# A two-layer hybrid trunk on one core: values and next scores of the samples in one stretch, spatial weights turned by VectorE, probabilities scaled by ScalarE

## The chip, the cores and the metric

The kernel runs as one program on one core of a Trainium2 chip. The metric is the device time of one execution in microseconds (us). The engines are named as in the profile: PE is TensorE (PEld its weight loads), DVE is VectorE, ACT is ScalarE, POOL is GpSimd, SP is SyncE, which issues most DMA transfers. Each engine works through its own list of instructions in order.

## What is computed

One inference step of a trunk with two layers, for a prompt (512 rows of 1024) and eight samples (16 rows each), all fp32. Layer 0 is a gated MLP whose mixing over positions works in blocks of 128 for the prompt and, for a sample, with the top left 16 x 16 of the same weights:

```
uv = gelu(h @ w_in[:, :2E]);  z = h @ w_in[:, 2E:]           # E = 2048
v  = layer_norm(uv[:, E:])
wm = where(chunk_causal, w_s[:, :n, :n], 0)                   # 16 groups, n = 128 or 16
s  = einsum('gij,bnjgc->bnigc', wm, v) + b_s
y  = (u * s * silu(z)) @ w_out
```

Layer 1 is attention with 16 heads of 128 and a cumulative forget bias. The prompt attends to itself; a sample attends to 256 cached rows and its own 16 rows:

```
s = q @ k.T * scale + c_q - c_k          # c = cumsum of log forget values
p = softmax(mask(s));  o = p @ v;  y = (o * silu(z)) @ w_out
```

Each layer ends with a norm, the residual, and a gated input embedding. Keys, values and log forget values of the new rows are outputs too.

## The kernel before

The 640 rows (512 of the prompt, 128 of the samples) are kept channel-major as two fp32r parts, high and low, and each large product is three fp32r products (lines 272 to 274): high by high, high by low, low by high. Weights are fetched into RAW tiles, and ACT writes the high part (line 289), DVE the low part (line 290, by subtraction). Many large products are done by a seven-product scheme (`seven_products`) whose sums of weights POOL makes (line 211).

Layer 0: panels of v (to about 120 us of the span), then eight pairs of channel groups (about 120 to 350 us). A pair g, g+1 runs the seven products for u, then `spatial_weights(g)` and `spatial_weights(g + 1)`, then the seven products for z, then `gate_spatial`, which multiplies v by the turned spatial weights. In `spatial_weights` the 128 x 128 weights of a group (`raw`) are turned by PE and copied by ACT into `wm` (lines 688, 690, 691). For the samples, DVE builds a matrix `ax` with the group's 16 x 16 weights (`w16`) eight times along the diagonal, PE turns it (line 689), and ACT copies it into `ws` (line 692). Behind every second of the first three pairs' ends, and before the first, a panel of v is normalised by ACT and DVE (`layer_norm_panel`).

Layer 1: eight rounds, one per pair of heads p. `interleave` walks through the seven-product steps of the next projections (z of p; v, k, q of p+1); a step adds 0.441 to a clock, and a piece of the attention of pair p is written into the program when the clock passes the number beside it. `sample_times`, `prompt_times` and `attention_pieces` are those tables. Behind them a scheduler of the compiler moves instructions within each engine's list by its own estimates; `tc.issue_after(x)` ties what is issued inside it behind x.

The samples' attention of a round goes in two groups `bg` of four samples. The pieces of a group: `scores` (eight products of 128 rows x 32 columns, four samples side by side on the four quarters of PE's columns, then the weighing: DVE adds the bias and takes the minimum, ACT the exponential, DVE the reciprocal and the masked copy of the new rows), `turn` (PE turns the probabilities), `values` (twelve such products, in the order of three key blocks t and four samples), `gate` (PE turns the output, DVE multiplies by z). The two groups use the same buffers: `pr` for probabilities and, over it, `os_` for the output; `kt` for keys and `vv` for values. `load_v(p, 1)` loads the values of the second group (512 KB twice) over those of the first. `bank(ATT)` hands out three PSUM banks in turn (4, 5, 6) to all attention pieces. `turn_v` turns the new values of the next pair (line 1071) into such banks.

The prompt's attention of a head has four query blocks, each with `scores`, `turn` (7.5 later), `values` (12.5 later). In `scores`, ACT takes the exponential (line 1175), DVE the reciprocal (line 1179), and DVE scales the probabilities (line 1180); `turn` has PE turn them (line 1186). `SML` holds one-column values; most are given out from a ring of 20, in layer 1 from a larger one.

## Time and profile before

| | |
|---|---|
| median of three runs | 1273.82 us (1273.16 to 1274.09) |
| profiled execution: its time | 1273.51 us |
| profiled execution: its span | 1271.6 us |
| PE busy | 1264.2 us (99%) |
| DVE busy | 957.1 us (75%) |
| ACT busy | 594.6 us (47%) |
| POOL busy | 356.2 us (28%) |
| granted TensorE clock | 1.000 |

The span runs from the first to the last instruction; what the time has beyond it (1.9 us) lies around it. The page lists groups of instructions by line of the kernel, engine, operation and tile, with the busy time, the mean of one in ns, and what ended the engine's idle time before them. A matmul's duration there reaches beyond the start of the next one, since matmuls are pipelined. In an order of time, a row has the start, the length from the first start to the last end of the merged rows, the engine, and how many records were merged. An fp32 product shows as two records, an fp32r product and a transpose as one.

### The profile page before, as it was taken

The numbers are of one execution on the slowest core, as the hardware profiler recorded it, in microseconds if no ns is written. First come the engines' busy times: TensorE is split into PE (matmuls) and PEld (weight loads), VectorE is DVE, ScalarE is ACT, GpSimd is POOL, SyncE is SP. The second block draws the span as 40 slices with busy tenths as digits, with TensorE's granted clock in tenths as the row PEclk, the third lists the DMA queues.
The fourth block names the chain that finished last, engine by engine and source line by source line (L and its number), as shares of the span: only waits on it lengthen the run. The fifth ranks groups of instructions, "written<-read, shape, count | busy, mean of one in ns | idle before, by whom it ended". The sixth has DMA issues, their size and how long they took to land.

```text
span 1271.6 us, 21433 instructions
## 1 busy us (share of the span) xinstructions
PE 1264.2 (99%) x8038; PEld 1136.5 (89%) x8038; DVE 957.1 (75%) x1795; ACT 594.6 (47%) x1076; POOL 356.2 (28%) x323
## 2 busy tenths in 40 slices
PE   9999999999999999999999999999999999999998
PEld 7888999999988888889999999999999998788887
DVE  6844999999953364789988998989898988545643
ACT  4433555544545343665445454545454445454331
POOL 1012445454000010145434535454435430000100
PEclk9999999999999999999999999999999999999999
DMA  5532343323324212657798858677888659632211
GB/s 201 174 98 78 108 127 112 103 80 104 114 94 144 94 44 84 150 127 157 173 167 168 195 150 186 157 172 142 151 168 179 177 110 283 230 129 84 67 66 50
DMA packets 275545, 171.54 MB, mean 135 GB/s; under 512 B 188721, under 2 KB 238689, under 8 KB 275442
## 3 DMA queue, kind: packets, MB, share of 16 engines
q1 hardware_dynamic: 261170, 127.80, 36.9%
q0 software_dynamic: 9760, 36.05, 13.7%
q10 hardware_dynamic: 4512, 6.33, 1.7%
q8 instruction: 63, 1.03, 0.3%
q14 instruction: 40, 0.33, 0.1%
HBM read 148.55 MB, written 21.59 MB: 134 GB/s over the span
## 4 chain that ended last, share of the span: by engine, by line
PE 97%; DVE 2%; issue 0%; ACT 0%; ACTq 0%; DVEq 0%
PE pb L272 27%; PE pb L274 27%; PE pb L273 27%; PE pb L1193 3%; PE pb L1270 2%; PE pb L419 2%; PE pb L1186 1%; PE pb L1243 1%; PE pb L317 1%; PE pb L745 1%; PE pb L1058 1%; DVE W L290 1%; PE pb L1071 1%; PE pb L1262 0%; PE pb L1059 0%
## 5 line engine op out<-in xcount | busy, mean ns | idle before, releaser
L272 PE MATMUL pb<-A,W 128*128 128x320 f32 (+1 forms) x752 | 240.7, 320 | 0.0
L273 PE MATMUL pb<-A,W 128*128 128x320 f32 (+1 forms) x752 | 233.7, 311 | 0.0
L274 PE MATMUL pb<-A,W 128*128 128x320 f32 (+1 forms) x752 | 233.2, 310 | 0.0
L290 DVE TENSOR_TENSOR W<-RAW,W 128x1024 fp32r<-128x1024 f32 (+1 forms) x122 | 149.6, 1227 | 71.9 <-ACT W L289 69.7
L273 PE MATMUL pb<-W,A 128*128 128x512 f32 x498 | 194.5, 391 | 0.0
L272 PE MATMUL pb<-W,A 128*128 128x512 f32 x498 | 194.5, 393 | 0.0
L274 PE MATMUL pb<-W,A 128*128 128x512 f32 x498 | 194.3, 391 | 0.0
L289 ACT ACTIVATE W<-RAW 128x1024 fp32r<-128x1024 f32 (+1 forms) x122 | 115.8, 949 | 90.0 <-PE pb L274 43.9
L272 PEld LDWEIGHTS pb<-A,W 128*128 128x128 f32 x752 | 141.6, 188 | 1.0 <-issue 0.2
L273 PEld LDWEIGHTS pb<-A,W 128*128 128x128 f32 x752 | 141.6, 188 | 0.5
L274 PEld LDWEIGHTS pb<-A,W 128*128 128x128 f32 x752 | 141.2, 188 | 0.0
L272 PE MATMUL pb<-tbf,W 128*128 128x320 f32 x360 | 118.9, 330 | 0.4 <-DVE R L1099 0.4
L303 POOL TENSOR_TENSOR SML<-SML 128x1 f32<-128x1 f32 x20 | 14.9, 749 | 350.9 <-DVE SML L301 346.2
L274 PE MATMUL pb<-tbf,W 128*128 128x320 f32 x360 | 111.3, 309 | 0.0
L273 PE MATMUL pb<-tbf,W 128*128 128x320 f32 x360 | 111.2, 309 | 0.0
L274 PEld LDWEIGHTS pb<-W,A 128*128 128x128 f32 x498 | 93.4, 188 | 19.6 <-issue 0.4
L273 PEld LDWEIGHTS pb<-W,A 128*128 128x128 f32 x498 | 93.6, 188 | 18.7
L272 PEld LDWEIGHTS pb<-W,A 128*128 128x128 f32 x498 | 93.5, 188 | 18.5
L211 POOL TENSOR_TENSOR sff<-RAW 128x512 f32<-128x512 f32 x46 | 61.2, 1330 | 169.3 <-DVE W L290 90.7
L713 DVE TENSOR_TENSOR R<-R,pb 128x320 f32<-128x320 f32 x184 | 86.3, 477 | 12.8 <-PE pb L274 11.7
L290 DVE TENSOR_TENSOR A<-R,A 128x640 fp32r<-128x640 f32 (+1 forms) x42 | 35.5, 880 | 57.8 <-ACT A L289 57.8
L272 PEld LDWEIGHTS pb<-tbf,W 128*128 128x128 f32 x360 | 67.7, 188 | 10.3 <-issue 5.8
(270 smaller groups left out, 2842.2 us busy)
## 6 DMA issues: line engine op xcount, KB each, us to landing
RAW<-in_fox_w_in POOLq DMA_DIRECT2D x46, 512.0 KB, 7.5
RAW<-in_gmlp_w_in SPq DMA_DIRECT2D x40, 512.0 KB
R<-in_cache_fox_k SPq DMA_DIRECT2D x128, 128.0 KB
R<-in_cache_fox_v SPq DMA_DIRECT2D x32, 512.0 KB
RAW<-in_gmlp_w_out SPq DMA_DIRECT2D x16, 512.0 KB
RAW<-in_ple_w_gate SPq DMA_DIRECT2D x16, 512.0 KB
RAW<-in_fox_w_out SPq DMA_DIRECT2D x16, 512.0 KB
R<-in_fox_w_in POOLq DMA_DIRECT2D x14, 512.0 KB, 8.5
```

The lines of the kernel that those rows point to most:

```text
L211: nc.gpsimd.tensor_tensor(out=o, in0=a, in1=b, op=op)
L272: nc.tensor.matmul(out, lh, rh, start=start, stop=False)
L273: nc.tensor.matmul(out, lh, rl, start=False, stop=False)
L274: nc.tensor.matmul(out, ll, rh, start=False, stop=stop)
L289: first = nc.scalar.activation(out=hi, in_=src, func=AF.Copy)
L290: nc.vector.tensor_tensor(out=lo, in0=src, in1=f(hi), op=ALU.subtract)
L303: behind["pool"] = nc.gpsimd.tensor_tensor(out=q, in0=t, in1=mhalf, op=ALU.pow)
L317: behind["pe"] = nc.tensor.transpose(out=b[:, j * P:(j + 1) * P], in_=src[:, (4 * c + j) * P:(4 * c + j + 1) * P], identity=ident)
L419: line[e] = make(*args, **kw)
L713: behind["dve"] = nc.vector.tensor_tensor(out=into(i, j), in0=a, in1=b, op=ALU.add)
L1193: nc.tensor.matmul(O[:, d], v[:, j, hh * P:(hh + 1) * P], pt[:, j * P:(j + 1) * P], start=(j == 0), stop=(j == i))
L1270: last = nc.tensor.matmul(O[32 * bl:32 * bl + 32, :256], pt[:, t * P + 32 * bl:t * P + 32 * bl + 32], v_of(p)[:, 4] if t == 2 else vv[:, b ...
```

## The change

Three edits.

1. Spatial weights of the samples: the 16 x 16 weights of all groups are loaded twice side by side (16 loads instead of 8), turned once for all groups by DVE, which turns blocks of 32 x 32, and the upper left of each block is copied by ACT into `w16`. `spatial_weights` then multiplies the turned weights by the block mask straight into `ws`; the transpose of `ax` and the copy behind it are gone.
2. Samples: `scores` is split into `products` (PE) and `weigh` (the rest). In rounds 0 to 6, `values` of group 0 moves to the time of the second group's scores and issues the second group's `products` in the same tied sequence; gate, `weigh` and `turn` of the second group follow. `load_v(p, 1)` moves from 18.5 to 26.1, `turn_v` from 26.0 and 27.0 to 28.7 and 29.7. The reciprocal gets a column of its own in `SML`. Round 7 keeps its order.
3. Prompt: the probabilities are scaled by ACT instead of DVE.

```diff
@@ spatial weights
+    twice, turned_twice = r1(o_u, 512), r1(o_u + 512, 512)
     for b in range(NB):
-        dma(w16[b * TS:(b + 1) * TS], w_s[0, :, :TS, :TS].rearrange("g i j -> i g j"))
+        for z in range(2):
+            dma(twice.rearrange("p (g z j) -> z p g j", g=16, z=2)[z, b * TS:(b + 1) * TS], w_s[0, :, :TS, :TS].rearrange("g i j -> i g j"))
+    with queued("dve"):
+        nc.vector.transpose(out=turned_twice, in_=twice)
+    nc.scalar.activation(out=w16, in_=turned_twice.rearrange("p (g z i) -> p g z i", g=16, z=2)[:, :, 0], func=AF.Copy)
...
-            out=ax.rearrange("p (b j) -> p b j", b=NB), in0=blk.rearrange("p (b j) -> p b j", b=NB),
+            out=ws.rearrange("p (b j) -> p b j", b=NB), in0=blk.rearrange("p (b j) -> p b j", b=NB),
...
-        nc.tensor.transpose(out=b[:, P:2 * P], in_=ax, identity=ident)
...
-        nc.scalar.activation(out=ws, in_=b[:, P:2 * P], func=AF.Copy)
@@ prompt scores
-            nc.vector.tensor_scalar(out=pr[:, :n], in0=pr[:, :n], scalar1=ri, scalar2=None, op0=ALU.mult)
+            nc.scalar.activation(out=pr[:, :n], in_=pr[:, :n], func=AF.Copy, scale=ri)
@@ samples
-        def scores():
-            S = bank(ATT)
+        def products(stack):
+            S = kept["S"] = bank(ATT)
+            for hh in range(2):
+                for bl in range(4):
+                    last = nc.tensor.matmul(S[32 * bl:32 * bl + 32, :272], qpads[:, hh, 4 * bg + bl].rearrange("p h q -> p (h q)"),
+                                            kt[:, hh, bl], start=(hh == 0), stop=(hh == 1))
+                    stack.enter_context(tc.issue_after(last.ins))
+
+        def weigh():
+            S = kept["S"]
...
-        def values():
+        def values(follow=None):
             O = bank(ATT)
             with ExitStack() as stack:
...
+                if follow is not None:
+                    follow(stack)
...
+        if p == 7:
+            return [(s0, scores), (s0 + 7.5, turn), (s0 + 12.5, values), (s0 + 17.5, gate),
+                    (s1, scores1), (s1 + 7.5, turn1), (s1 + 12.5, values1), (s1 + 17.5, gate1)]
+        return [(s0, scores), (s0 + 7.5, turn), (s1, lambda: values(products)), (s1 + 2.5, gate), (s1 + 2.6, weigh),
+                (s1 + 7.5, turn1), (s1 + 12.5, values1), (s1 + 17.5, gate1)]
...
-                   (s0 + kb + 0.1, lambda: new_k(p, 1)), (s0 + 13.5, lambda: load_v(p, 1))]
+                   (s0 + kb + 0.1, lambda: new_k(p, 1)), ((s0 + 13.5 if p == 7 else s1 + 0.1), lambda: load_v(p, 1))]
...
-        pieces += [(26.0, lambda p=p: turn_v(p + 1, 0)), (27.0, lambda p=p: turn_v(p + 1, 1))]
+        pieces += [(28.7, lambda p=p: turn_v(p + 1, 0)), (29.7, lambda p=p: turn_v(p + 1, 1))]
```

How the built programs stand on PE is shown at three places. First, a round of layer 1 (the second one) before, where the first group's values stand: line 1270 is the values, line 1186 the turning of a prompt block's probabilities, lines 272 to 274 the large products, `pb_N` a PSUM bank.

```order
L274 MATMUL pb_71<-A,W 128x320
L1270 MATMUL pb_74<-R_69 32x256 x4
L1186 MATMUL pb_76<-CST,R_69 128x128 x2
L1270 MATMUL pb_74<-R_69 32x256 x8
L272 MATMUL pb_72<-tbf,W 128x320
```

The same round before, some 70 rows later, where the second group's scores stand (line 1243; line 1193 is the prompt's values, line 1071 `turn_v`):

```order
L274 MATMUL pb_72<-A,W 128x320
L1193 MATMUL pb_77<-R_69 128x128 x3
L1243 MATMUL pb_74<-R_69 32x272 x8
L1071 MATMUL pb_75<-CST,R_69 128x128 x4
L272 MATMUL pb_73<-tbf,W 128x320
```

And that round now, where both stand together (line 1282 is the values, 1244 the scores, 1189 the turning, 1196 the prompt's values):

```order
L274 MATMUL pb_72<-A,W 128x320
L1282 MATMUL pb_75<-R_69 32x256 x10
L1189 MATMUL pb_74<-CST,R_69 128x128 x4
L1282 MATMUL pb_75<-R_69 32x256 x2
L1244 MATMUL pb_76<-R_69 32x272 x8
L272 MATMUL pb_72<-A,W 128x320
L273 MATMUL pb_72<-A,W 128x320
L274 MATMUL pb_72<-A,W 128x320
L1196 MATMUL pb_77<-R_69 128x128 x3
```

The values moved to the scores' place. They were cut after four by two transposes and are cut after ten by four now; the eight scores follow the last two values with nothing between, in all of rounds 0 to 6. `turn_v` (line 1074 now) stands later, twice four transposes into banks 74 and 76, the second of which is the scores' bank.

In layer 0, one of sixteen places where the transpose of the samples' weights stood, as a difference:

```order
 L273 MATMUL pb_71<-A,W 128x320
 L274 MATMUL pb_71<-A,W 128x320
-L689 MATMUL pb_74<-CST,R_69 128x128
 L272 MATMUL pb_71<-A,W 128x320
 L273 MATMUL pb_71<-A,W 128x320
```

The row is gone, and nothing takes its place on PE.

More of the change, by code (lines that the diff above doesn't have):

```diff
@@ L74, in hybrid_trunk @@
     CST = sbuf.tile([P, C_N], F32, name="CST")
-    SML = sbuf.tile([P, N_SMALL], F32, name="SML")
+    SML = sbuf.tile([P, N_SMALL + 2], F32, name="SML")
     R1 = sbuf.tile([P, N_R1], F32, name="R1")
@@ L681, in spatial_weights @@
         z = g % 2
-        raw, wm, ws, ax = r1(o_wsr + z * P, P), r1(o_wm + z * P, P), r1(o_ws + z * P, P), r1(o_ax, P)
+        raw, wm, ws = r1(o_wsr + z * P, P), r1(o_wm + z * P, P), r1(o_ws + z * P, P)
         nc.vector.scalar_tensor_tensor(out=spb[z], in0=spb[z], scalar=lnb[:, g:g + 1], in1=r1(o_bs + z * P, P), op0=ALU.mult, op1=ALU.add)
         nc.vector.tensor_tensor(
-            out=ax.rearrange("p (b j) -> p b j", b=NB), in0=blk.rearrange("p (b j) -> p b j", b=NB),
+            out=ws.rearrange("p (b j) -> p b j", b=NB), in0=blk.rearrange("p (b j) -> p b j", b=NB),
             in1=w16[:, g:g + 1, :].broadcast_to([P, NB, TS]), op=ALU.mult)
@@ L1235, in sample_pieces @@
         kept = {}
-        def scores():
-            S = bank(ATT)
+        def products(stack):
[7 more added lines that the diff above has]
+            S = kept["S"]
             with queued("dve"):
                 nc.vector.tensor_tensor(out=Wc[:, PAST:], in0=Wc[:, PAST:], in1=CST[:, C_M16:C_M16 + TS], op=ALU.add)
-            for hh in range(2):
-                for bl in range(4):
-                    nc.tensor.matmul(S[32 * bl:32 * bl + 32, :272], qpads[:, hh, 4 * bg + bl].rearrange("p h q -> p (h q)"),
-                                     kt[:, hh, bl], start=(hh == 0), stop=(hh == 1))
-            m, sm, ri = small(), small(), small()
+            m, sm, ri = small(), small(), SML[:, N_SMALL + bg:N_SMALL + bg + 1]
             nc.vector.tensor_tensor_reduce(out=pr[:, :272], in0=S[:, :272], in1=Wc, scale=1.0, scalar=3e38, op0=ALU.add,
@@ L1263, in turn, with scores @@
             nc.scalar.activation(out=pt, in_=tb[:, :384], func=AF.Copy)
-        def values():
+        def scores():
+            with ExitStack() as stack:
+                products(stack)
+            weigh()
+        def values(follow=None):
             O = bank(ATT)
@@ L1285, in gate @@
                                                op0=ALU.mult, op1=ALU.mult)
-        return scores, turn, values, gate
+        return scores, turn, values, gate, products, weigh
     def prompt_times(h, t0, step):
@@ L1296, in prompt_times, with sample_times @@
         return res
-    def sample_times(p, bg, t0):
-        scores, turn, values, gate = sample_pieces(p, bg)
-        return [(t0, scores), (t0 + 7.5, turn), (t0 + 12.5, values), (t0 + 17.5, gate)]
+    def sample_times(p, s0, s1):
+        scores, turn, values, gate, _, _ = sample_pieces(p, 0)
+        scores1, turn1, values1, gate1, products, weigh = sample_pieces(p, 1)
+        if p == 7:
[3 more added lines that the diff above has]
+                (s1 + 7.5, turn1), (s1 + 12.5, values1), (s1 + 17.5, gate1)]
     def store_y(h):
@@ L1319, in attention_pieces @@
         s0, t0 = 5, 4
-        pieces = sample_times(p, 0, s0) + sample_times(p, 1, s1)
+        pieces = sample_times(p, s0, s1)
         ka, kb = 5, 17.6
         pieces += [(s0 + ka, lambda: turn_k(p, 1, 0)), (s0 + ka + 0.1, lambda: load_k(p, 1, 1)), (s0 + kb, lambda: turn_k(p, 1, 1)),
-                   (s0 + kb + 0.1, lambda: new_k(p, 1)), (s0 + 13.5, lambda: load_v(p, 1))]
+                   (s0 + kb + 0.1, lambda: new_k(p, 1)), ((s0 + 13.5 if p == 7 else s1 + 0.1), lambda: load_v(p, 1))]
         for hh in range(2):
```

## The prediction

> **What bounds the kernel now.** I read the page's busy times first, then a table by stage, then what TensorE waits for, and last the order of time around the places that the change touches.
>
> ```profile
> PE 1264.2 (99%) x8038; PEld 1136.5 (89%) x8038; DVE 957.1 (75%) x1795; ACT 594.6 (47%) x1076; POOL 356.2 (28%) x323
> 120.00:350.00 230.00, 229.53 (x1583) 226.78 (x1582) 215.44 (x337) 119.41 (x218) 93.52 (x61) 1.00 0.35 109
> 575.00:1052.00 477.00, 477.00 (x3645) 447.18 (x3644) 421.94 (x974) 229.70 (x456) 214.13 (x207) 1.00 0.77 164
> PEld pb L272 <- DVE R L726: 1.3, 3, 0.4
> ```
>
> The two window rows are the gMLP products (120 to 350 us) and the seven attention rounds (575 to 1052 us); after the length stand the busy times of PE, PEld, DVE, ACT and POOL, then the clock, the DMA share and GB/s. PE is busy for 229.53 of 230 and for 477.00 of 477 us at full clock. So the path is TensorE's own list of instructions: an instruction taken off it shortens the kernel, one put on it lengthens it, and a lighter VectorE by itself gives nothing. VectorE is the next one (215.44 of 230, 421.94 of 477), so a late VectorE is the way to lose. A busy PE can hide an array that is slowly fed; therefore I price everything from the distance between starts, not from durations.
>
> **Edit 1: spatial weights turned by VectorE.** It takes 16 transposes off TensorE (line 689) and 16 copies off ScalarE (line 692).
>
> ```profile
> 143.54 0.31 PE L272 MATMUL pb<-tb,W 128*128 128x320 f32 x1
> 143.98 0.31 PE L272 MATMUL pb<-A,W 128*128 128x320 f32 x1
> 144.13 0.27 PE L689 MATMUL pb<-CST,R 128*128 128x128 f32 x1
> 144.53 0.31 PE L272 MATMUL pb<-A,W 128*128 128x320 f32 x1
> L689 PE MATMUL pb<-CST,R x16: 270/270/272, 140.8 to 336.4; 128*128 128x128 f32 x16
> L692 ACT ACTIVATE R<-pb x16: 277/278/280, 141.6 to 338.0; 128x128 f32<-128x128 f32 x16
> ```
>
> From 143.54 to 143.98 three products take 0.44 us (0.147 each); from 143.98 to 144.53 three products and one transpose take 0.55. A transpose thus costs 0.11 us, not its 0.27 of duration, and 16 of them 1.8 us. The copies (16 x 0.278 = 4.4 us) come off a ScalarE that is busy 119 of 230 us and give nothing by themselves.
>
> What it adds:
>
> ```profile
> 62.80 1.82 SPq L124 DMA_DIRECT2D R<-in_gmlp_w_s  x4
> 69.45 0.33 SPq L124 DMA_DIRECT2D R<-in_gmlp_b_s  x1
> 75.53 0.38 SPq L124 DMA_DIRECT2D RAW<-in_gmlp_w_in  x1
> 125.61 0.16 DVE L649 SCALAR_TENSOR_TENSOR SML<-SML 128x1 f32<-128x1 f32 x1 [0.66 <-POOL SML L303]
> L1219 DVE STREAM_TRANSPOSE R<-R x128: 395/403/444, 559.7 to 1074.9; 128x256 f32<-128x256 f32 x128
> L1085 DVE STREAM_TRANSPOSE R<-R 128x640 f32<-128x640 f32 x16 | 13.3, 831 | 0.0
> ```
>
> Eight more loads on SP's queue at 1.82/4 = 0.46 us are 3.6 us; that queue is free from 69.8 to 75.53, so the weight load behind them stays on time, and the data are there some 50 us before VectorE wants them near 125 us. One VectorE transpose of 128x512 lies between the 128x256 row (0.40) and the 128x640 row (0.83): about 0.7 us, once, standing before the last statistics, where VectorE had 0.66 us idle. If that cover is gone it is 0.7 us in all. The ScalarE copy of 128x256 is less than half a microsecond beside PE's products. Taken: 0, with 0 to 0.7 for the range.
>
> The weight loads of PE wait in this stage three times for VectorE behind the normalisation panels, 1.3 us in all (the wait quoted first). The VectorE work there is the same and starts from PE, so it moves along with PE. At worst each of the three swallows the 0.2 us that its pair of transposes gave (0.7 us in all). Taken: 0.
>
> **Edit 2: values and next scores in one stretch.** Both are products on a quarter of the array (128*32), four side by side.
>
> ```profile
> 667.70 0.31 PE L274 MATMUL pb<-A,W 128*128 128x320 f32 x1
> 667.94 0.64 PE L1270 MATMUL pb<-R 128*32 128x256 f32 x8
> 668.51 0.44 PE L1186 MATMUL pb<-CST,R 128*128 128x128 f32 x2
> 668.88 1.07 PE L1270 MATMUL pb<-R 128*32 128x256 f32 x16
> 669.88 0.41 PE L272 MATMUL pb<-tbf,W 128*128 128x320 f32 x1
> 670.13 0.31 PE L273 MATMUL pb<-tbf,W 128*128 128x320 f32 x1
> ...
> 681.88 1.12 PE L1243 MATMUL pb<-R 128*32 128x272 f32 x16
> 682.94 0.66 PE L1071 MATMUL pb<-CST,R 128*128 128x128 f32 x4
> 699.85 1.50 PE L1270 MATMUL pb<-R 128*32 128x256 f32 x24
> 701.28 0.41 PE L272 MATMUL pb<-tbf,W 128*128 128x320 f32 x1
> ```
>
> A product here is two records, so x24 is twelve products, six passes deep on each of the four column groups. By starts, x8 lasts 0.57, x16 1.00 and x24 1.43 us: 0.215 a pass and 0.14 once per stretch. Going in costs 0.24 - 0.15 = 0.09. Coming out, the first big product is 0.25 - 0.15 = 0.10 longer. Between two stretches stand two transposes of 0.11 in 0.37 us, 0.15 too many, of which 0.09 is the way in again, so coming out into a transpose costs 0.06. A stretch that ends in transposes is therefore 0.09 + 0.14 + 0.06 = 0.29 us beside its passes. The scores at 681.88 are such a stretch (1.06 us, four passes of 0.23).
>
> Before, a round has five stretches: scores, four values, eight values, scores, values. The new order has four, as the scores of the second group stand right behind the values: 0.29 us saved in each of seven rounds. But the tie does not keep other work out: the values are cut after ten, four transposes come in, and two values follow. Before, the cut lay after four, one value per column group. After ten, groups 0 and 1 have three values (six passes), groups 2 and 3 two; the transposes need the whole array, so they wait for six passes. Behind them groups 2 and 3 still owe two passes each, and their scores stand behind these, while groups 0 and 1 have scores alone: six passes instead of four. Is it the longest group that counts? The forget logits show it:
>
> ```profile
> 540.85 0.84 PE L968 MATMUL pb<-R,WF 128*32 128x128 f32 x24
> 541.63 1.09 PE L317 MATMUL pb<-CST,R 128*128 128x128 f32 x8
> ```
>
> By line 968's loop these twelve products are three of 128 columns in group 3, two each in groups 0 and 1, five of 64 in group 2. With a pass of 128 columns at half of 0.215, group 3 takes 6 x 0.108 = 0.65, plus 0.14 = 0.79 us; the rows show 0.78. The even share would be 0.63. So the longest group sets the end, and the cut costs 2 x 0.215 = 0.43 us a round. Net 0.43 - 0.29 = 0.14 longer, seven times 1.0 us. The eighth round is not tied.
>
> The Trainium skill, "TensorEngine Tiling (Array Packing)", section "Key Properties", says that a change of tiling mode drains the engine; the rows agree with the price just read. Counting changes alone by that rule, the edit would be worth -7 x 0.29 = -2.0 us instead of +1.0; that is the second rival below.
>
> Moved with it: the values' load of the second group (1 MB) is now issued behind the next pair's keys.
>
> ```profile
> R<-in_cache_fox_v SPq DMA_DIRECT2D x32, 512.0 KB
> 669.98 0.94 SPq L124 DMA_DIRECT2D R<-in_cache_fox_v  x2
> 677.99 9.01 SPq L124 DMA_DIRECT2D R<-in_cache_fox_k  x4
> 687.10 3.20 SPq L124 DMA_DIRECT2D out<-R  x5
> ```
>
> On this clock it leaves near 687.1 rather than 669.98, and is read at 699.85: 12.7 us. At the stage's 164 GB/s 1 MB takes 6.4 us, so 6 us are left; sharing the engines with another 1 MB of weights it would take all of them. Taken: 0; late by at most 1 us a round. Behind it on SP stand the stores of values and the next keys, which move back by about 1 us of issue; these keys are turned 12 of the planner's units after their load.
>
> **Edit 3: probabilities scaled by ScalarE.**
>
> ```profile
> L1180 DVE TENSOR_SCALAR R<-R,SML 128x128 f32<-128x128 f32 (+1 forms) x64 | 36.4, 568 | 0.8
> L1175 ACT ACTIVATE R<-R,SML 128x128 f32<-128x128 f32 (+1 forms) x64 | 35.7, 558 | 73.8 <-DVE SML L1172 73.8
> L1188 ACT ACTIVATE R<-pb 128x128 f32<-128x128 f32 (+1 forms) x64 | 27.2, 426 | 24.6 <-PE pb L1186 23.2 <-issue 1.3
> L1179 DVE RECIPROCAL SML<-SML 128x1 f32<-128x1 f32 x64 | 10.0, 157 | 10.8 <-ACT R L1175 10.4
> L290 DVE TENSOR_TENSOR W<-sff,W 128x1024 fp32r<-128x1024 f32 x44 | 53.8, 1223 | 9.9 <-ACT W L289 9.9
> ```
>
> VectorE loses 64 x 0.568 = 36.4 us. ScalarE gains 64 copies of the same four widths: 0.43 us as in its copies from PSUM to 0.56 as in its exponentials, 27 to 36 us, on 230 busy of 477. PE covers both. The new wait: a scaling stands in ScalarE's list behind its exponential and needs VectorE's reciprocal, so the weight halves and copies behind it wait too; a reciprocal that has just missed its turn is one 1.22 us subtraction late. The planner sets the transposes of the probabilities 7.5 of its units behind their scores, six such subtractions, even at 1 us a unit. Taken: 0.
>
> **The sum.** The profiled execution took 1273.51 us, 0.3 below the median of 1273.82. -1.8 + 1.0 = -0.8 gives 1272.7 for it, and **1273.0 us** against the median: no change that can be told. The likeliest case's own range is 1272.0 to 1274.5: up to 0.7 each for the new VectorE transpose and the three waits, and as much downwards if these three shorten.
>
> **Rivals.**
> First, **slower: the third score bank is late.** The second group's scores now lie in their bank until the first group's output has been turned, since the weighing writes over that output. The transposes of the new values into this bank (line 1071 before) come 18 products and six transposes later, 3.3 us. In between are two gate products on VectorE and the weighing:
>
> ```profile
> L1284 DVE SCALAR_TENSOR_TENSOR R<-pb,R 128x64 f32<-128x64 f32 x32 | 5.6, 214 | 0.8 <-PE pb L1278 0.8
> L1246 DVE CUSTOM_DVE_ANT_0 R<-pb,R 128x272 f32<-128x272 f32 x16 | 6.9, 434 | 3.8 <-PE pb L1243 3.8
> ```
>
> 0.22 for the turning, 0.43 and 0.51 with its read make 1.2 us, so 2 us are spare. If VectorE or ScalarE is behind by 2.5 us there (two weight subtractions of 1.22), PE stands 0.5 us a round, and that is the point: 3.5 us in seven rounds outweigh the 0.8. With three or four subtractions it is 1.7 to 2.9 a round; I price it at 0.8 a round, 1273.0 + 5.6 = 1278.6. For it: VectorE's 421.94 of 477, and a ScalarE that now waits for VectorE 64 times more. Against: VectorE gets lighter, and PE lost nothing in this stage to the same kind of waits. The Trainium skill, "TensorE: Matmul & The Clock Gate", section "Architectural detail: the array is 16× 32×32, not 1× 128×128", calls the queues of ScalarE and VectorE strict first-in first-out; the 73.8 us that ScalarE idles before its exponentials agree. Chance 0.15.
>
> Second, **faster: the cut costs nothing**, as when the two late values slip in front of the transposes: -1.8 - 2.0 = -3.8, 1270.0. Against it the rows at 667.94 to 668.88, where the cut stands as written, and the logits. Chance 0.08.
>
> Third, the values' load is late by up to 1 us a round: up to 1280. It needs both transfers at once. Chance 0.03.
>
> Forecast: 0.74. About 0.2% (2.5 us) is what a measurement of this kernel can tell from no change; so faster 0.09 (the second rival and a little chance), slower 0.16 (the first, and the third where it is late by over half a microsecond), same 0.75. Range 1271.0 to 1276.5: it leaves out the second rival and the far ends of the slower ones.
>
> **What would show it.** No transposes of the spatial mixing at sixteen places, PE's stage 0.11 us shorter for each. In each of seven rounds ten values lasting 1.43 us by starts, four transposes, then two values with the scores in 1.45 to 1.5 us to the next big product. PE busy 477 in the rounds still, with no wait on VectorE at the transposes of the values. Wrong would be: that last stretch near 1.05 us, any wait of PE in the rounds above 0.3 us that comes back seven times, or a ScalarE list that holds weights back.

## The result, and the profile after

The change makes the kernel slower: 1284.72 us (1284.28 to 1286.14) against 1273.72 us (1273.16 to 1274.09) of the kernel before beside it, a ratio of 1.009 with an interval of 1.008 to 1.010. The forecast was 1273.0, in a range of 1271.0 to 1276.5: it was wrong, by 11.7 us. The profiled execution took 1284.28 us, its span is 1282.4 us where it was 1271.6, so 10.8 us have to be found.

The page's busy times and its chain by engine, after:

```profile
PE 1267.6 (99%) x8022; PEld 1136.2 (89%) x8022; DVE 937.7 (73%) x1732; ACT 623.0 (49%) x1125; POOL 350.1 (27%) x323
PE 88%; DVE 8%; issue 2%; ACT 1%; DMA 0%; ACTq 0%; DVEq 0%
```

The chain before:

```profile
PE 97%; DVE 2%; issue 0%; ACT 0%; ACTq 0%; DVEq 0%
```

The gMLP products and the attention rounds in the view by windows, after:

```profile
120.00:350.00 230.00, 228.08 (x1565) 225.07 (x1564) 216.88 (x336) 116.65 (x203) 91.11 (x61) 1.00 0.36 109
575.00:1052.00 477.00, 470.74 (x3582) 439.88 (x3581) 398.75 (x908) 253.35 (x508) 208.53 (x208) 1.00 0.80 163
```

The 16 transposes are gone (8038 matmuls before, 8022 now) and VectorE's work in the rounds fell from 421.94 to 398.75 us. But PE, which was busy for all of 477 us of the rounds, now stands for 6.3 of them, and VectorE has 8% of the chain where it had 2%. What PE waits for, in the view of waits after, in the rounds and then in the gMLP stage:

```profile
PE pb L1244 <- DVE SML L1175: 2.9, 5, 1.2
PE pb L1189 <- ACT R L1183: 1.9, 2, 1.7
PE pb L272 <- DVE SML L1175: 1.5, 1, 1.5
```

```profile
PE pb L272 <- DVE R L727: 1.2, 2, 0.6
```

Line 1244 is the products of the tied scores, line 1175 VectorE's minimum over the prompt's scores, line 1189 the turning of the prompt's probabilities, line 1183 ScalarE's scaling.

Where in time the 10.8 us went is read from the start of the same instruction in both traces: the first group's scores of a round (line 1243 before, 1244 after). Before, for rounds 0, 1 and 2:

```profile
585.06 1.12 PE L1243 MATMUL pb<-R 128*32 128x272 f32 x16
652.81 1.12 PE L1243 MATMUL pb<-R 128*32 128x272 f32 x16
720.56 1.12 PE L1243 MATMUL pb<-R 128*32 128x272 f32 x16
```

After:

```profile
586.08 1.12 PE L1244 MATMUL pb<-R 128*32 128x272 f32 x16
659.38 0.90 PE L1244 MATMUL pb<-R 128*32 128x272 f32 x12
727.22 1.12 PE L1244 MATMUL pb<-R 128*32 128x272 f32 x16
```

Round 0 begins 1.0 us late and ends 6.6 us late; round 1 adds 0.1. Layer 0 is read at the first product of its eight pairs and at the first product behind them. Before:

```profile
124.29 0.30 PE L272 MATMUL pb<-A,W 128*128 128x320 f32 x1
343.99 0.48 PE L272 MATMUL pb<-W,A 128*128 128x512 f32 x1
```

After:

```profile
123.36 0.30 PE L272 MATMUL pb<-A,W 128*128 128x320 f32 x1
343.42 0.48 PE L272 MATMUL pb<-W,A 128*128 128x512 f32 x1
```

The changed kernel is 0.9 us ahead at 124 us, but not by the change: the lead arises in the first 11 us, in instructions that all the kernels here share, and in the traces of the runs below it lies anywhere from 0.2 to 1.4 us, with and without edit 1. The eight pairs themselves take 220.06 us where they took 219.70. By the same readings at every stage:

| stage | later (+) by, us |
|---|---|
| start of the kernel (to 124 us) | -0.9 |
| pairs of the gMLP (124 to 344) | +0.4 |
| rest of layer 0 with its tail (344 to 585) | +1.6 |
| first attention round | +5.6 |
| rounds 1 to 6 | +0.1, +0.75, +0.75, +0.75, +0.1, +0.3 |
| last round and last tail | +1.4 |

The two tails do what they did before, yet about 1.4 us are lost in each. The groups of products that take their stationary operand from the tiles r2x_t (layer 0) and r2z_t (layer 1) show why; the columns after the count are the shortest, median and longest duration in ns. Before:

```profile
L272 PE MATMUL pb<-W,r2x_t x80: 387/389/398, 464.1 to 528.2; 128*128 128x512 f32 x80
L272 PE MATMUL pb<-W,r2z_t x88: 277/389/397, 1204.1 to 1266.6; 128*128 128x512 f32 x72, 128*128 128x256 f32 x16
```

After:

```profile
L272 PE MATMUL pb<-W,r2x_t x80: 392/395/403, 463.5 to 529.1; 128*128 128x512 f32 x80
L272 PE MATMUL pb<-W,r2z_t x88: 277/395/400, 1213.5 to 1277.4; 128*128 128x512 f32 x72, 128*128 128x256 f32 x16
```

Each lasts 6 ns longer (from start to start 232 to 233 ns where it was 227), in 240 and 216 products of 512 columns: 1.4 and 1.3 us. And in round 0 VectorE waits for a transfer that it never waited for before, the samples' mask:

```profile
584.54 1.18 DVE L1251 TENSOR_TENSOR R<-R,CST 128x16 f32<-128x16 f32 x1 [2.32 <-DMA R<-cs_sc]
```

Before, the same instruction ran at once:

```profile
581.13 0.16 DVE L1240 TENSOR_TENSOR R<-R,CST 128x16 f32<-128x16 f32 x1
```

VectorE's list runs in order, so it falls behind from there, and PE stands 1.5 us until 600.1, 1.7 until 605.5 and 1.2 until 619.3 us for work of VectorE and ScalarE.

### The profile page after: what moved, and what is told of

Its sections match the earlier page's. It is cut to its first block, busy times and chain, and to the rows that moved or that the text cites. A ratio compares the mean times of both kernels' runs of the same rounds, so it can differ in the third digit from the quotient of the medians.

```text
span 1282.4 us, 21349 instructions
## 1 busy us (share of the span) xinstructions
PE 1267.6 (99%) x8022; PEld 1136.2 (89%) x8022; DVE 937.7 (73%) x1732; ACT 623.0 (49%) x1125; POOL 350.1 (27%) x323
## 4 chain that ended last, share of the span: by engine, by line
PE 88%; DVE 8%; issue 2%; ACT 1%; DMA 0%; ACTq 0%; DVEq 0%
PE pb L272 25%; PE pb L274 25%; PE pb L273 25%; PE pb L1196 3%; DVE W L290 2%; PE pb L419 2%; PE pb L1244 1%; PE pb L1282 1%; PE pb L1189 1%; PE pb L317 1%; DVE R L1222 1%; PE pb L748 1%; DVE R L716 1%; PE pb L1061 1%; DVE R L1126 1%
## 5 line engine op out<-in xcount | busy, mean ns | idle before, releaser
L1178 ACT ACTIVATE R<-R,SML 128x128 f32<-128x128 f32 (+1 forms) x64 | 35.9, 561 | 90.5 <-DVE SML L1175 90.4
```

What stands on the lines that cost most here:

```text
L1178: nc.scalar.activation(out=pr[:, :n], in_=pr[:, :n], func=AF.Exp, scale=-1.0, bias=m, accum_out=sm)
```

## The experiments

A line of the change that the prediction passed over is the suspect for both: SML got two more columns for the kept reciprocals. In the built program R1, which is laid out behind SML, then starts at byte 117,280 of a partition instead of 117,248, a multiple of 256; the second tile behind it (r2x_t, r2z_t and others) at 188,320 instead of 188,288, a multiple of 128. The theory to start from: these 32 bytes, a wait of the tie's products for their bank, and new waits in the gMLP stage make the 10.8 us. The rival: the tie's moved loads and ScalarE's longer list cost the first round. The ratios stand on several executions each, and single ones scatter: of 31 executions of the kernel before, taken beside four of the later runs, 28 took 1272.2 to 1274.8 us and three 1275.5 to 1281.9.

**The addresses alone.** The kernel before with

```diff
-    SML = sbuf.tile([P, N_SMALL], F32, name="SML")
+    SML = sbuf.tile([P, N_SMALL + 2], F32, name="SML")
```

> The kernel before with one edit only: the tile SML gets two more columns that nothing uses, as in the change. The order of all instructions stays what it was; only the addresses of R1 and of the tiles behind it move by 8 bytes. Address theory: the 512-wide products of the two tails, which the changed kernel's trace shows at 232 to 233 ns from start to start where they took 227 before, are slowed by those 8 bytes; then they take 232 here too (225 and some 210 of them, 1.3 us each tail), and the time is 1273.7 + 2.7 = 1276.4 us. Rival: they are slow in the changed kernel for another reason (what runs beside them); then 227 ns and 1273.7 us here.

Measured: 1281.45 us (1279.11 to 1284.80) against 1273.41, ratio 1.0060 (1.0037 to 1.0084). Two columns that nothing uses cost not 2.7 but some 8 us. The tails are as the theory says (their group of products here):

```profile
L272 PE MATMUL pb<-W,r2x_t x80: 392/395/403, 463.9 to 529.5; 128*128 128x512 f32 x80
```

And round 0 loses too; its waits of VectorE for transfers and of PE for VectorE:

```profile
DVE R L1240 <- DMA R<-cs_sc: 1.7, 1, 1.7
PE pb L1186 <- DVE R L1180: 2.7, 1, 2.7
```

SP's DMA queue here, with packets, MB, and the share of the 16 DMA engines' time:

```profile
q1 hardware_dynamic: 261170, 127.80, 38.7%
```

Before, the same packets and bytes took less:

```profile
q1 hardware_dynamic: 261170, 127.80, 36.9%
```

The trace's packet records say which: the 172,032 packets of 128 bytes, most of them of the key cache, whose rows go into R1 in pieces of 128 bytes. Their mean is 13.0 ns before and 15.0 here; nine tenths took at most 13 ns before, at most 21 here. Packets of 512, 1024 and 2048 bytes are within 1.2 ns of 30 to 101 before. With R1 at 32 bytes past a multiple of 256, every second piece of 128 bytes crosses such a multiple, and none did before. The Trainium skill, "DMA: Bandwidth & Descriptors", section "How a descriptor splits into AXI transactions", says that a transaction on the bus must start at a multiple of 256 bytes, and that for a piece which does not start at one the bytes between the multiple below it and its start cost bus time too. The direction agrees; the page speaks of bytes fetched, while here the odd address is where they are written, and how large the effect is, 2 ns in 13, only the trace tells. The mask is loaded while these packets run: its last packet landed at 577.4 us before and at 583.7 here, where VectorE wants it at 581 and 582.6. The Trainium skill, same page, section "Issuing engines are not separate DMA queues", says that transfers issued by different engines run on the same 16 DMA engines and interleave. That R1's address delays the mask is seen over the traces of all runs: its first packet comes at 579.1 to 580.3 us in the three with R1 off a multiple of 256, and at 573.6 to 575.2 us in the seventeen others.

Which of the two tiles does what is told apart by the kernel before with R1 longer by 32 bytes:

```diff
-    N_R1 = 17760
+    N_R1 = 17768
```

> The kernel before with R1 wider by eight columns (32 bytes) that nothing uses: SML and R1 start where they did, only the tiles behind R1 (the operands of the tails, the weights' second buffers) move by 32 bytes; order unchanged. If the products of the tails are slow by where their stationary operand lies, and the loads by where R1 lies, then the tails take 232 ns a product (+2.7 us in all), while the 128-byte packets stay at 13 ns and the first round loses nothing: 1276.1 us. Rival: the loads and the first round suffer by what lies behind R1: 1281.

Measured: 1277.02 us (1275.81 to 1278.40) against 1273.67, ratio 1.0022 (1.0012 to 1.0032).

```profile
L272 PE MATMUL pb<-W,r2x_t x80: 392/395/403, 462.8 to 528.4; 128*128 128x512 f32 x80
```

```profile
q1 hardware_dynamic: 261170, 127.80, 37.1%
```

The products of the tails are slow, the 128-byte packets are at 13.0 ns again. So the stationary operand's address costs the tails 2.7 us, and R1's address costs the transfers. The profiled execution still lost 1.2 us in round 0 with the mask 1.1 us late; the median is 0.9 us above the expected 1276.1, and this remainder isn't explained by the packets.

Would 64 bytes do? The change with

```diff
-    SML = sbuf.tile([P, N_SMALL + 2], F32, name="SML")
+    SML = sbuf.tile([P, N_SMALL + 16], F32, name="SML")
```

> The changed kernel with SML widened by sixteen columns (64 bytes) in place of two; the order of all instructions is that of the changed kernel. Address theory: the 512-wide products of the tails are back at 227 ns and the time is 1284.7 - 2.7 = 1282.0 us. Rival (another reason than the address): 232 ns and 1284.7 us.

Measured: 1281.54 us (1280.97 to 1282.73), ratio 1.0060 (1.0044 to 1.0076); the tails' products still at 233 ns, the packets at 14.6. The expected time came out, for the wrong reason: 64 bytes past a multiple of 128 slow the products as 32 do, and the addresses were not mended. Its trace lost 2.6 us in round 0 where the change lost 5.6; why is open.

**The edits one by one,** with SML as it was. Edit 1 alone:

> Edit 1 alone (spatial weights turned by VectorE), SML as before. Up to the attention its order is that of the changed kernel. If the two new waits of 0.83 us behind the transposes at 187.0 and 215.5 us belong to this edit, they stand here too and the edit is worth -1.76 + 2 x 0.83 + 3 x 0.09 = +0.2, with the rest of the gMLP stage measured at -0.5 in all: 1273.2 to 1273.9 us. Rival: they come from addresses or chance, then the transposes give their 1.8 us: 1272.0. For the round-0 loss of 5.5 us: if it comes with this edit (a mask that lands later because everything ahead moved), 1279; I expect it does not.

Measured: 1276.87 us (1274.38 to 1279.76) against 1273.41, ratio 1.0023 (1.0011 to 1.0035). The trace has the two new waits in the gMLP stage (at 186.6 and 215.0 us, 0.88 each). It begins the attention 1.0 us ahead, but it was 1.4 ahead at the first product of the pairs already; the pairs are 0.3 us longer here as well. VectorE's list in the changed kernel, which is the same there, shows what makes PE wait. Before:

```profile
168.86 0.68 DVE L290 TENSOR_TENSOR W<-R,W 128x512 fp32r<-128x512 f32 x1
169.86 0.98 DVE L684 TENSOR_TENSOR R<-CST,R 128x128 f32<-128x128 f32 x1
```

After:

```profile
166.65 0.28 DVE L689 TENSOR_TENSOR R<-CST,R 128x128 f32<-128x128 f32 x1
168.27 1.72 DVE L290 TENSOR_TENSOR W<-R,W 128x512 fp32r<-128x512 f32 x1 [0.20 <-ACT W L289]
```

The second multiplication by the block mask (line 684, 689 now) stands ahead of the subtraction now, not behind it, and the subtraction lasts 1.72 us here and near 197 and 225 us in every trace with edit 1, 0.68 in every trace without it. It now begins 0.12 us behind a sum on GpSimd (168.15); before, it began 0.16 us ahead of one (169.02). That this is the reason is not shown.

The larger loss of edit 1 comes behind that, in rounds whose order this edit doesn't touch:

```profile
DVE R L729 <- DMA out<-R: 1.2, 1, 1.2
DVE R L1243 <- DMA R<-cs_sc: 1.0, 1, 1.0
PE pb L1189 <- DVE R L1183: 1.7, 2, 1.2
```

VectorE waits for the mask and for a store of fresh keys or values (it writes where the store still reads), and PE for VectorE. So a part of the first round's loss does come with this edit, which the expectation didn't expect, though the packets here are at 13.0 ns. This is taken up below.

Edit 3 alone (the one line of the prompt's scaling):

> Edit 3 alone (prompt probabilities scaled by ScalarE), SML as before; every load stands in the same order as before. If the losses in the attention rounds (5.5 us in the first, 0.58 in four more) come from ScalarE's longer list, they are here too: up to 1273.7 + 7.8 = 1281.5 us, with waits of PE on VectorE's line 1175 or ScalarE's line 1183. If they come from the tie (its loads moved on SP, its products' bank), this edit costs nothing: 1273.4 to 1274.0, and no wait of PE in the rounds above 0.3 us beside the old one at 1052.6.

Measured: 1272.65 us (1271.59 to 1279.39) against 1273.41, ratio 1.0000 (0.9984 to 1.0016). It costs nothing and PE shows no wait in the rounds: ScalarE's longer list isn't what loses.

Edit 2 alone, with the reciprocals kept in two unused columns of R1 so that all addresses stay:

```diff
-            m, sm, ri = small(), small(), SML[:, N_SMALL + bg:N_SMALL + bg + 1]
+            m, sm, ri = small(), small(), r1(o_w1 + P + bg, 1)
```

> The tie alone (samples' values and next scores in one stretch), with the addresses of the kernel before; the scaling stays on VectorE and the spatial weights on TensorE. If the tie's products wait for their bank by the order of banks (the prompt's first scores still being read by VectorE), 0.58 us in some rounds is here too: 1273.4 + 1.0 + 2.3 = 1276.7 us, and more where VectorE, which keeps its 36 us of scaling, is later still. Rival: the wait comes from ScalarE's scaling, which holds VectorE up; then only the cut is left: 1274.4.

Measured: 1284.40 us (1280.88 to 1290.17) against 1273.67, ratio 1.0091 (1.0055 to 1.0127), worse than either theory:

```profile
PE pb L1186 <- DVE R L1180: 6.0, 4, 1.5
PE pb L1241 <- DVE SML L1172: 2.0, 4, 0.5
```

The wait for the bank is there (line 1241 is the products, line 1172 the minimum that reads the bank), in four rounds. But the scheduler left the stretch together in no round here: three large products, the four transposes of the prompt's last block and two products of its values stand between the twelve values and the eight scores. These transposes wait in the same four rounds for VectorE, which keeps its 36 us of scaling, 1.5 us each time. So this run is not the change less two edits, and that the tie needs edit 3 is not shown by it.

**The whole change with the old addresses,** by the same line as above in the changed kernel; the order of all instructions is the changed kernel's.

> The whole change, but the two kept reciprocals stand in two columns of R1 that nothing else uses, and SML has its old width: the order of all instructions is that of the changed kernel, the addresses of R1 and of what lies behind it are those of the kernel before. Address theory: everything that the widening alone cost goes (products of the tails back from 232 to 227 ns, packets of 128 bytes back to 13 ns in the mean, no wait for the mask in the first round); left are -0.5 us in the gMLP stage and 7 x 0.14 + 4 x 0.58 = +3.3 us in the rounds: 1273.4 - 0.5 + 3.3 = 1276.2 us. Rival: the first round's loss (5.5 us) comes from the loads that the tie moves on SP; then it stays and the time is 1281.7.

Measured: a profiled execution of 1275.98 us, close to the expected 1276.2, with the tails at 227 ns, the packets at 13.0 and no loss in round 0; but a median of 1281.49 (1275.98 to 1284.37) against 1273.67, ratio 1.0053 (1.0038 to 1.0067). The theory holds for the execution that was profiled, and most others are 4 to 8 us later. Once more, to see another execution:

> The whole change with the old addresses once more, to see an execution of the slower sort. Its first run gave 1276.0 us in the profiled execution and a median of 1281.5. Mask theory: a slower execution shows VectorE waiting for the mask of the first round, and PE standing 1 to 3 us around 600 us. Keys theory: it shows VectorE waiting for keys at 655 to 666 us, and PE standing up to 5 us near 665, as one execution of the run with the later first mask did.

Measured: 1280.00 us (1276.20 to 1282.77) against 1273.87, ratio 1.0045 (1.0030 to 1.0060). The profiled execution, again near the fast end (1276.82), shows the mask 1.6 us late and round 0 0.9 us longer than in the trace at 1275.98. If the mask is the cause, a mask that is wanted later must help:

```diff
-        s0, t0 = 5, 4
+        s0, t0 = (5 if p else 8), 4
```

> The whole change with the old addresses, and in the first round alone the samples' scores of the first group are set 3 of the planner's units later (8 in place of 5), so that VectorE's mask addition stands 11 instructions later in its list. The run with old addresses was profiled at 1276.0 us without any wait in the first round, while its other executions reached 1284.4. Mask theory: in these the mask, which landed at 577 to 582 us in the profiles so far while VectorE wants it near 581, came too late, and VectorE's list and then PE stood; with 3 us more the executions gather near the fastest one: median 1276 to 1277.5 us. Rival: the spread has another source (weights or keys later in the rounds); then the median stays near 1281.

> The whole change with old addresses and the first mask 3 units later once more, beside the run without that shift on the same chip. Mask theory: median 1277 to 1278 us, some 4 us below that run. Keys theory: the same median as that run, 1280 or more.

Measured: 1277.67 us (1276.55 to 1285.90), ratio 1.0035 (1.0012 to 1.0058), and 1278.74 (1276.49 to 1285.65), ratio 1.0043 (1.0022 to 1.0063), the second on the same chip as the 1280.00 above. Eight of ten and six of ten executions gather below 1279.1, the others lie at 1282.4 to 1285.9. In the two runs without the shift it was two and four of ten. On the one chip the medians differ by 1.3 us, less than either run scatters, so that the mask is a part is likely and not shown; it is not all, since late executions remain. A profiled execution of the late sort (1285.60) shows the other part:

```profile
DVE R L1222 <- DMA R<-in_cache_fox_k: 8.3, 2, 7.7
PE pb L272 <- DVE SML L1175: 5.1, 2, 4.9
```

The keys of round 1 landed 7.7 us after VectorE wanted them, and PE stood 4.9 us. Such a stop can cost more than its length, since the clock granted to TensorE may fall behind it. In the view by windows (the clock is the third figure from the end), from this trace:

```profile
667.40:674.20 6.80, 3.74 (x14) 3.74 (x15) 6.80 (x14) 2.18 (x6) 4.63 (x3) 0.52 0.55 97
```

Products of 320 columns start 0.27 us apart behind this stop, 0.147 elsewhere; an estimated 1.7 us are lost by that until 674.2. The profiled execution of the change has no such stretch: its clock is 1.00 throughout, with stops of up to 1.7 us. The same shift in the kernel before:

> The kernel before with the first round's sample scores 3 units later, nothing else. If the mask is what sometimes disturbs the kernel before as well (executions of 1275 to 1278 us among many at 1273), its executions gather at 1272.5 to 1273.5. Rival: they stay spread, or the later scores cost something of their own: 1273.5 or more.

Measured: 1276.52 us (1274.69 to 1278.05) against 1273.61, ratio 1.0023 (1.0013 to 1.0033): the later scores cost 3 us of their own there. The shift is no remedy.

**Why does the spatial edit hurt the rounds?** It leaves two candidates: its eight more loads of 16 KB, or all that it does to the engines. The loads alone, in the kernel before:

```diff
         dma(w16[b * TS:(b + 1) * TS], w_s[0, :, :TS, :TS].rearrange("g i j -> i g j"))
+        dma(r1(o_u, 512).rearrange("p (g z j) -> z p g j", g=16, z=2)[0, b * TS:(b + 1) * TS], w_s[0, :, :TS, :TS].rearrange("g i j -> i g j"))
```

> The kernel before with eight more small loads of the spatial weights (into columns that are overwritten later), which nothing uses; transposes and copies as before. Loads theory: the eight loads change how all later transfers fall on the DMA engines, so that the mask or the keys of the first rounds come late in more executions: median 1276 to 1277 us, executions from 1274 to 1280, as with the spatial edit alone. Rival (what counts is that PE and VectorE reach the first round 1 us earlier, or VectorE's work): 1273.6 us, as before.

And the whole edit without them, the second half of each block copied by GpSimd:

```diff
-        for z in range(2):
-            dma(twice.rearrange("p (g z j) -> z p g j", g=16, z=2)[z, b * TS:(b + 1) * TS], w_s[0, :, :TS, :TS].rearrange("g i j -> i g j"))
+        dma(twice.rearrange("p (g z j) -> z p g j", g=16, z=2)[0, b * TS:(b + 1) * TS], w_s[0, :, :TS, :TS].rearrange("g i j -> i g j"))
+    halves2 = twice.rearrange("p (g z j) -> z p g j", g=16, z=2)
+    nc.gpsimd.tensor_copy(out=halves2[1], in_=halves2[0])
```

> The spatial edit alone, but with eight loads as in the kernel before: the second half of each block comes from a copy on GpSimd. Loads theory: the edit's gain shows, 1272.6 to 1273.1 us in the median, with the kernel before's spread. Rival (the lead of PE): 1276 to 1277 us, as with the spatial edit alone.

Measured side by side, the kernel before at 1273.72: the loads alone 1278.48 us (1274.20 to 1282.21), ratio 1.0029 (1.0013 to 1.0044); the edit without them 1274.44 (1272.93 to 1278.07), ratio 1.0001 (0.9987 to 1.0015). What VectorE waits for among transfers, and PE for VectorE, with the loads alone (lines stand one further than in the kernel before):

```profile
DVE R L727 <- DMA out<-R: 2.6, 1, 2.6
DVE R L1220 <- DMA R<-in_cache_fox_k: 1.8, 2, 1.1
PE pb L272 <- DVE SML L1173: 2.1, 1, 2.1
```

Behind PE's stop of 2.1 us the clock falls here too, for 3.4 us:

```profile
598.80:602.20 3.40, 3.40 (x16) 3.40 (x15) 3.40 (x4) 1.51 (x5) 3.24 (x3) 0.53 0.43 67
```

The profiled execution of the edit without the loads shows no wait of VectorE for a transfer in the rounds. So the eight loads, which are over at about 70 us, raise the median by some 4 us, with no instruction of PE, VectorE or ScalarE added, and the trace shows VectorE waiting for transfers near 587 and 663 us. Such waits are not peculiar to the loads: two traces below without the spatial edit have them too (1.2 to 2.2 us), in executions of 1272.7 and 1272.9 us. How the loads reach that far is open: the records don't tell which of the 16 engines carried a packet, and no run here separates it. The edit itself, without them, gains nothing that can be measured.

**The tie, earlier and later.** All with the old addresses. Earlier:

```diff
-        pieces = attention_pieces(p, 4.8, 26.0) + next_keys(p + 1, 34.0, 46.2)
+        pieces = attention_pieces(p, 4.8, 25.4) + next_keys(p + 1, 34.0, 46.2)
```

> As the run with old addresses (whole change, SML at its old width), but the tied stretch starts at 25.4 of the planner's units in place of 26.0: the four transposes of the prompt's probabilities no longer fall into it (twelve values and eight products stand together), and the products get another bank, not the one that holds the prompt's first scores. By the prices read from the trace before, the cut (0.43 us) and the wait (0.58 us) both go and each of seven rounds gains 0.29: 1273.4 - 0.5 - 2.0 = 1270.9 us. Rival: the tie saves nothing even uncut, or the products wait for the new bank too: 1273 or more.

Measured: 1276.35 us (1271.50 to 1277.95) against 1273.67, ratio 1.0012 (0.9999 to 1.0025), 5 us below the same change at 26.0. Two executions reach 1271.5, near the expected 1270.9; the profiled one of them still has a wait, which moved:

```profile
PE pb L1189 <- DVE SML L1175: 2.3, 5, 0.5
```

The products no longer take the bank of the prompt's first scores; the four transposes of the prompt, next in turn, do, and wait for VectorE in its place. Later, with the first mask 3 units later as well:

```diff
-        pieces = attention_pieces(p, 4.8, 26.0) + next_keys(p + 1, 34.0, 46.2)
-        pieces += [(28.7, lambda p=p: turn_v(p + 1, 0)), (29.7, lambda p=p: turn_v(p + 1, 1))]
+        pieces = attention_pieces(p, 4.8, 27.5) + next_keys(p + 1, 34.0, 46.2)
+        pieces += [(30.2, lambda p=p: turn_v(p + 1, 0)), (31.2, lambda p=p: turn_v(p + 1, 1))]
```

> As the run before this one (whole change, old addresses, first mask 3 units later), and the tied stretch starts at 27.5 of the planner's units in place of 26.0, the transposes of the new values 1.5 later too: the four transposes of the prompt stand ahead of the stretch, not in it, and the products still take the bank of the prompt's first scores, but seven products of 0.147 us (1.0 us) later. If the 0.58 us of waiting was for VectorE's reading of that bank, it is gone, and the cut (0.43) with it: 1276.2 - 2.3 - 3.0 = 1270.9 us. Rival: the transposes of the prompt now wait for ScalarE's scaling, 0.6 us in five rounds as in the run with the early tie: 1273.9.

Measured: 1273.26 us (1272.04 to 1279.81) against 1273.61, ratio 1.0004 (0.9989 to 1.0018). The order of time at one of these stretches:

```profile
749.69 1.50 PE L1282 MATMUL pb<-R 128*32 128x256 f32 x24
751.01 1.10 PE L1244 MATMUL pb<-R 128*32 128x272 f32 x16
752.04 0.42 PE L272 MATMUL pb<-tbf,W 128*128 128x320 f32 x1
```

Twelve values and eight products take 2.35 us without a cut and without a wait for the bank. Other waits of PE remain, of 0.2 to 0.9 us: for VectorE in round 0, for ScalarE in round 1 and near 1052 us. The same without the spatial edit, with the later and with the old first mask, and the whole with the old first mask:

> As the run with the late tie (tie at 27.5, ScalarE's scaling, first mask 3 units later, old addresses), but the spatial weights as in the kernel before. By the gMLP stage of the traces (-1.0 to -0.5 us net for the VectorE transposes) it should be 0.5 to 1.0 us above that run: 1271.4 to 1271.9 us. Rival: the transposes' removal sets the rest 1 us earlier against its loads and costs more than it gives; then this run is the faster one.

> The tie at 27.5 units and ScalarE's scaling, old addresses, spatial weights as before, the first mask at its old place. The run with the first mask later gave 1271.8. If the later first scores cost something of their own, as they did in the kernel before (1276.5 against 1273.6), this one is at 1270 to 1271; if the mask is late here too, 1274 or more.

> All three edits with old addresses and the tie at 27.5 units, the first mask at its old place. Against the run at 26.0 units beside it, the uncut tie should give 0.43 us in seven rounds and the wait 0.58 in four, 5.3 us in all. Against the run without the spatial edit: 0.5 to 1.0 us less, or, if the spatial edit makes the first mask and the keys late, up to 4 us more.

| late tie, old addresses | spatial edit | first mask | median, us | ratio to the kernel before |
|---|---|---|---|---|
| e11_late | yes | later | 1273.26 | 1.0004 (0.9989 to 1.0018) |
| e13_no1 | no | later | 1271.77 | 0.9986 (0.9973 to 0.9998) |
| e16_no1late5 | no | as before | 1272.27 | 0.9984 (0.9965 to 1.0002) |
| e17_late5 | yes | as before | 1277.58 | 1.0042 (1.0014 to 1.0071) |

With the spatial edit the kernels are 1.5 and 5.3 us slower than without it; that agrees with its loads. Without it the late tie and ScalarE's scaling come to 1.6 to 1.8 us less than the kernel before: the best of this study, at the edge of what can be measured. With the old addresses, the tie moved and the spatial edit left out, nothing of the 11 us is left.

## Why the prediction was wrong

Point by point, by its own steps; the largest failure is a term that it put at nothing without saying so, the two columns of SML:

- **"a transpose thus costs 0.11 us ... 16 of them 1.8 us"** was right for PE: at each of the sixteen places its list is 0.11 us shorter. But the pairs came out 0.3 to 0.4 us longer. Where a panel of v is normalised, VectorE's list is full and sets the time, and it fell behind: its line 683 (688 now) begins 1.06 us earlier than before, at 164.82, and line 724 (727 now) only 0.29 earlier, at 187.33. PE then stood twice (0.84 and 0.87 us), and three old waits grew by 0.1 each: 2.0 us, where the bound given for this was "0.7 us in all". The sentence "the VectorE work there is the same and starts from PE, so it moves along with PE" is the one that failed. The work is the same, but it stands in another order and takes longer there, as shown with edit 1 alone.
- **"Net 0.43 - 0.29 = 0.14 longer, seven times 1.0 us"** was right. Ten values lasted 1.42 us by starts (1.43 forecast), the stretch of two values and the scores 1.47 ("1.45 to 1.5"), and a round without another wait is 0.10 us longer, as rounds 1 and 5 show. The longest column group does set the end. Uncut, the tie does save: 67.53 us from round 2 to round 3 in the late tie's trace against 67.75, so 0.22 of the 0.29 us.
- **The third bank** was a rival at 0.15, and its kind was right: VectorE late on a score bank. The two late values and the scores last 2.12 us in four rounds and 2.88 in the first, 1.47 without the wait: 0.65 and 1.4 us. Its place was wrong. I asked who comes behind the scores' bank (the turned values) and not who was in it before: the ring of three hands the products the bank of the prompt's first scores, and they wait for VectorE's reading of that (line 1175).
- **"Taken: 0" for ScalarE's scaling** was right (ratio 1.0000, interval 0.9984 to 1.0016).
- **"Eight more loads on SP's queue ... 3.6 us; that queue is free"** priced them where they are issued. No run shows a cost there; 500 us on, in the first two rounds, they come to some 4 us in the median (1278.48 against 1273.72).
- **The two columns of SML** were not priced at all. They are the largest item: some 8 us by themselves (1281.45 against 1273.41), 2.7 in the tails and the rest by late transfers in the first rounds. Taken out of the change they gave back only 3.2 and 4.7 us in the median (1281.49 and 1280.00 of 1284.72), so the costs of the single edits can't simply be added.
- **"PE lost nothing in this stage"** was read as slack. The mask's last packet landed at 577.4 us, 3.7 us before VectorE wanted it, the last piece of round 1's keys at 653.3, 5.7 us before; the page shows waits, and not how near a transfer is to becoming one.

In the change's own profiled execution the sum is then: start -0.9, pairs 0.4, tails 2.7 (shown by two runs with the address alone and one with it undone), first round 5.6, the other rounds 2.75 (the cut 0.6, the bank 2.6, less 0.44 of a wait near 1052 us that the kernel before has and the change has not), 0.25 over the rest. In the first round 1.4 us stand at the bank. The address alone lost 3.2 us in round 0 in its profiled execution; how the rest of the 5.6 divides between the address, the eight loads and the tie's moved loads was not separated, since the three act on the same transfers.

## What to carry to other kernels

A tile that is widened moves every tile behind it: look up the addresses of the built program before and after, and put a new small buffer where nothing moves. Where a ring of banks gets a new taker, ask who held that bank before it and which engine still reads it, not only who comes next. And a transfer that lands just in time shows no wait in the profile: compare its landing with the time at which it is wanted, since any more traffic or a slower packet turns it into one that an in-order engine hands on to all the others. Before a lead is put down to an edit, look whether it was there ahead of the first instruction that the edit touches.

## What was not expected of the hardware

- Products of 512 columns whose stationary operand (128 x 128, fp32r) starts 32 or 64 bytes past a multiple of 128 take 232 to 233 ns from start to start, and 227 ns at a multiple of 128; the weight loads' own durations stay at 188 ns in the median. The products of 320 columns that stream their operand from a tile which moved by the same 32 bytes (tb, tbf) stayed at 147 ns.
- Packets of 128 bytes into rows that start 32 or 64 bytes past a multiple of 256 take 14.6 to 15.0 ns in the mean, 13.0 at a multiple.
- Behind stops of PE of 4.9, 2.1 and 1.5 us, in the late execution above, with the eight loads alone and with edit 2 alone, the granted clock fell to half for 6.8, 3.4 and 3.4 us. It did not behind the change's stops of 1.5 and 1.7 us, nor behind three more stops of the same 1.5 us with edit 2 alone; no rule is to be read from this.
- Eight loads of 16 KB at about 60 to 70 us change how late the transfers near 600 us land, in a kernel of otherwise the same order. The cause stays open.
